# Binding eight partition-sum products into one row, and moving the keys' transposes, in a two-layer hybrid inference step

## The chip, the cores and the metric

The kernel runs on one core of one Trainium2 chip. The metric is the device time of one launch in microseconds (us). The program's matrix engine is called PE or TensorE here, its vector engine DVE or VectorE, its activation engine ACT, its fourth compute engine POOL; SP issues most transfers from the chip's memory.

## What is computed

Two layers are applied to 128 context tokens (g = 0) and 128 latent tokens (g = 1) of width 2048. Cut to what matters:

```python
# mod = silu(c) @ w_mod[l] + b_mod[l]: six segments of 2048 columns,
# for each of two conditioning vectors (context, latent)
shift1, scale1, gate1, shift2, scale2, gate2 = split(mod, 6)
h = rmsnorm(x, norm1) * (1 + scale1) + shift1
proj = h @ w_in            # attention q, k, v; linear attention q, k, v, gates
# attention: per-head RMS norm of q and k, rotary positions, softmax
# gated linear attention (GLA), forward and backward, in chunks
x = x + gate1 * (concat(att, gla) @ w_out)
h = rmsnorm(x, norm2) * (1 + scale2) + shift2
x = x + gate2 * (square(relu(h @ w_up)) @ w_down)
```

## The kernel before

**Main work.** Everything is float32. A weight matrix is worked on in blocks of 512 columns (`block`, lines 398 to 453); a block takes 256 rows of the weights at a time (a chunk). SP loads a chunk, ACT casts it to a rounded high part `wh` (line 131), DVE subtracts to get the low part `wl` (line 132; both are called `wx` where they live in a borrowed buffer), and PE adds three products per 128 rows and token group: lines 443, 444 and 445, the third being the only one that reads the low part. A chunk has twelve such main matmuls of 128x512. The results are finished by `done`, and other work is put between the chunks as `side` steps.

**Modulation.** The twelve segments of `mod` come from 12 matrices of 2048x2048, one column of which meets two conditioning vectors only. Most segments go through PE (`mod_pe`, line 293). Five are accumulated on DVE by `mod_dve` (lines 339 to 367): (0,5), (1,1), (1,0) and (1,2) during layer 0 and (1,5) during layer 1, written (layer, segment). For each half of the columns and each group of 128 rows, DVE multiplies the loaded block `rawm` by that row's conditioning value and adds it to two sums `ga` of 128x1024, one per token group (lines 355 and 357): 32 blocks, 64 such instructions a segment. The four sums lie in borrowed buffers QT, KT, BF, BB, which the next segment uses again. What is left is the sum over the partitions:

```python
for g in range(2):
    for q in range(4):
        nc.tensor.matmul(ps[32 * q:32 * q + 32, :], unit[:, 1 - g:33 - g],
                         acc[q // 2][g][:, (q % 2) * 512:(q % 2) * 512 + 512], start=g == 0, stop=g == 1)
```

Eight products of PE (line 364), each taking two passes, so 16 matmuls in the trace, with a 128x32 weight tile `unit` that puts the sum of group g into row g of a quarter of the result. q = 0, 1 belong to the first half of the columns, whose sums are complete 16 blocks earlier than those of q = 2, 3.

**Keys.** `kv_a` is called when a block of keys and values is finished, once for each token group; it norms and (for the latent tokens) rotates the keys `y` (lines 744 to 756, DVE and POOL), transposes them on PE (line 769, tile `kaT`) and copies the result with ACT into `kTp` or `kTs`, which the attention reads later. The block after that is the queries' projection `Q_A`, whose side steps are two levels of the GLA (`level`, line 708's small matmuls `sc`).

**Order.** Each engine has its own queue. Where nothing else is said, a scheduler in the compiler decides the order in it from a simulated timeline, so that an edit in one place can move instructions elsewhere. `tc.high_priority()` puts an instruction ahead of others that are ready; `after(x, others)` adds an order without a semaphore.

**The boundary of the layers.** After layer 0's last block, `norm` (lines 460 to 476) forms the next layer's input: a chain of one-column operations (`v` line 138 on DVE, `y` twice on ACT lines 140 and 141, `t` twice on DVE lines 143 and 144, `r` line 146), a diagonal tile `dg` (line 469), 16 products with it on PE (line 473, `xnT`), and evictions by `modulate` (`xv` lines 482 and 484, then high part TH and low part TL, lines 131 and 132). Layer 1's first matmuls read TH and TL.

Of the kernel before, what the change touches and what calls it, by code (L numbers as in the profile page):

```python
# [20 lines left out]
P = 128  # L21
# [6 lines left out]
Q_A, K_A, Q_G, K_G, V_G, O_G, R_F = 0, 1024, 1536, 2048, 2560, 3584, 4608  # L28
# [23 lines left out]
def trunk(tc, nc, I, O):  # L52
    with ExitStack() as st:
# [41 lines left out]
        def mtile(shape=(P, 512), name="m"):  # L95
            return ps_m.tile(list(shape), F32, tag="m", name=name)
# [171 lines left out]
        shared = [lambda: rawp.tile([P, 1024], F32, tag="raw", name="rawm")]  # L268


        main = []

        def mod_group(ps, todo, size, behind={}):

# [68 lines left out]
        def mod_dve(l, seg):  # L343
            acc = []
# [14 lines left out]
                    if half < 1 or kc < KC - 1:  # L359
                        yield 1  # L360
            ps = mtile((P, 512), "mod")
            for g in range(2):
                for q in range(4):
                    nc.tensor.matmul(ps[32 * q:32 * q + 32, :], unit[:, 1 - g:33 - g],  # L364
                                     acc[q // 2][g][:, (q % 2) * 512:(q % 2) * 512 + 512], start=g == 0, stop=g == 1)
            mod_columns(l, seg, ps, 1)
            yield 1

# [31 lines left out]
        def block(TH, TL, src, at=None, done=None, mods_per=0.0, chs=None, side=(), dve=None, early={}):  # L400
# [14 lines left out]
            for g, ch in order:  # L415
# [23 lines left out]
                for k in range(2):  # L439
                    kc = ch * 2 + k  # L440
                    first, final = ch == chs[0] and k == 0, ch == chs[-1] and k == 1
                    xh, xl = TH[:, kc, g * P:(g + 1) * P], TL[:, kc, g * P:(g + 1) * P]
                    nc.tensor.matmul(acc[g], xh, wh[:, k, :], start=first, stop=False)  # L443
                    nc.tensor.matmul(acc[g], xl, wh[:, k, :], start=False, stop=False)  # L444
                    m = nc.tensor.matmul(acc[g], xh, wl[:, k, :], start=False, stop=final)  # L445
                    if len(main) < 16:
                        main.append(m)
                if ch == chs[-1] and done is not None:
# [110 lines left out]
        for l in range(L):  # L559
# [203 lines left out]
                nc.scalar.copy(x, pt)  # L763

            def kv_a(g, y):
                x = qk_finish(y[:, 0:256], 2, 1, g)
                pt = mtile((P, 2, P), "kaT")
                for j in range(2):
                    nc.tensor.transpose(pt[:, j], x[:, j], ident)
                if g == 0:  # L770
                    store(O["new_cache_k"][0, l], x)
                    store(O["new_cache_v"][0, l], heads(y[:, 256:512]))
                    nc.scalar.copy(kTp, pt)
                else:
                    nc.scalar.copy(kTs[:, :, P:2 * P], pt)

            MH, ML = new_t()

# [32 lines left out]
            att = lambda g, kv: lambda: attend(g, kv, heads(QA[kv][:, g]), heads(KA[:, g, 256:512]))  # L811
            QA = [None, None]
            KA = proj(K_A, kv_a, side=lv[0:2])
            QA[0] = proj(Q_A, q_a, side=lv[2:4])
            in_turn(shared)
            mod_rate[0] = N_MOD["bc"[l]][1]
            QA[1] = proj(Q_A + 512, q_a, side=[att(0, 0), lv[4], att(1, 0), lv[5]])
# [215 lines left out]
```

## Time and profile before

| | |
|---|---|
| Time, median of 3 runs (lowest to highest) | 2346.33 us (2345.97 to 2348.18) |
| Profiled execution: its time, and the span of its records | 2340.4 us, 2338.6 us |
| Mean granted clock of TensorE | 0.993 |
| Busy: PE, DVE, ACT, POOL | 2294.8, 1629.2, 1091.2, 187.5 us |
| Read from memory, written | 601.01 MB, 10.03 MB |

Busy times count an engine's own instructions. A row of a timeline gives start, duration, engine, line, operation, out<-in, and behind it in brackets the idle time of that engine just before it and what ended that; matmuls follow each other in a pipeline, so their durations overlap, and the step from start to start is what one costs. "PEld" is PE's weight load.

### The profile page before, as it was taken

What the parts mean: (1) busy time and instruction counts of PE and PEld (TensorE: products, weight loads), DVE (VectorE), ACT (ScalarE), POOL (GpSimd) and SP (SyncE); (2) the same over time, 40 slices, a digit from 0 to 9 for tenths busy, and PEclk for the clock granted to TensorE, in tenths of its full rate; (3) what the DMA queues carried; (4) which work ended last, traced back from release to release, by engine and by line L of the source; (5) the groups of instructions that cost most, each with busy time, mean ns of one, the idle gap of its engine ahead of it and who ended that gap; (6) DMA issues with size and microseconds to landing.
All of it is one profiled execution on the core that took longest, in us unless ns stands there. A gap on an engine that the chain in (4) does not pass through costs nothing.

```text
span 2338.6 us, 34912 instructions
## 1 busy us (share of the span) xinstructions
PE 2294.8 (98%) x13603; PEld 1830.4 (78%) x13603; DVE 1629.2 (70%) x1935; ACT 1091.2 (47%) x1476; POOL 187.5 (8%) x260
## 2 busy tenths in 40 slices
PE   8999899999999999999999999999999999999998
PEld 5677577788788788788777677788888888888887
DVE  4656767589999999589874865567996454445455
ACT  4334446455445344435454554546544543543542
POOL 1001521000000000000010522010000000000010
PEclk8999999999999999999999999999999999999999
DMA  9999889869989898588887667776887656656673
GB/s 351 376 344 351 292 280 357 299 215 308 312 289 320 283 318 287 203 272 298 277 292 263 203 231 229 255 256 225 296 292 236 182 190 196 180 193 193 181 232 134
DMA packets 278374, 613.35 MB, mean 262 GB/s; under 512 B 24368, under 2 KB 32880, under 8 KB 278208
## 3 DMA queue, kind: packets, MB, share of 16 engines
q1 hardware_dynamic: 268128, 581.51, 73.6%
q0 software_dynamic: 9872, 29.53, 4.3%
q8 instruction: 107, 1.75, 0.3%
q14 instruction: 59, 0.48, 0.1%
q10 hardware_dynamic: 208, 0.08, 0.0%
HBM read 601.01 MB, written 10.03 MB: 261 GB/s over the span
## 4 chain that ended last, share of the span: by engine, by line
PE 90%; DMA 3%; issue 2%; DVE 2%; ACT 1%; POOL 0%; SPq 0%; POOLq 0%; DVEq 0%; ACTq 0%
PE acc L443 27%; PE acc L445 26%; PE acc L444 26%; PE mod L293 4%; DMA rawm<-in_w_mod_dram 2%; DMA bank<-in_w_mod_dram 1%; PE aT L125 1%; PE xnT L473 1%; PE sc L708 1%; PE mod L364 1%; DVE wl L132 1%; PE po L806 0%; PE op L869 0%; PE mod L239 0%; PE op L866 0%
## 5 line engine op out<-in xcount | busy, mean ns | idle before, releaser
L132 DVE TENSOR_TENSOR wl<-raw,wh 128x1024 fp32r<-128x1024 f32 (+1 forms) x586 | 692.1, 1189 | 429.3 <-ACT wh L131 421.4
L131 ACT CAST wh<-raw 128x1024 fp32r<-128x1024 f32 (+1 forms) x586 | 593.4, 1017 | 780.4 <-PE acc L444 673.1
L443 PE MATMUL acc<-wh,TH 128*128 128x512 f32 x2248 | 887.5, 395 | 5.5 <-ACT TH L131 3.1
L444 PE MATMUL acc<-wh,TL 128*128 128x512 f32 x2248 | 881.2, 392 | 0.1
L445 PE MATMUL acc<-wl,TH 128*128 128x512 f32 x2248 | 862.8, 394 | 0.3 <-DVE wl L132 0.3
L443 PEld LDWEIGHTS acc<-wh,TH 128*128 128x128 f32 x2248 | 423.6, 188 | 105.0 <-issue 10.3
L445 PEld LDWEIGHTS acc<-wl,TH 128*128 128x128 f32 x2248 | 422.5, 188 | 95.7 <-issue 6.2
L444 PEld LDWEIGHTS acc<-wh,TL 128*128 128x128 f32 x2248 | 423.7, 188 | 87.5 <-issue 1.1
L357 DVE SCALAR_TENSOR_TENSOR ga<-rawm,CT,ga 128x1024 f32<-128x1024 f32 x300 | 377.1, 1277 | 25.1 <-DMA rawm<-in_w_mod_dram 24.7
L132 DVE TENSOR_TENSOR wx<-raw,wx 128x1024 fp32r<-128x1024 f32 (+1 forms) x182 | 194.6, 1079 | 88.9 <-ACT wx L131 86.7
L131 ACT CAST wx<-raw 128x1024 fp32r<-128x1024 f32 (+1 forms) x182 | 168.3, 938 | 177.6 <-PE acc L444 144.7
L444 PE MATMUL acc<-wx,TL 128*128 128x512 f32 x632 | 246.1, 390 | 0.0
L443 PE MATMUL acc<-wx,TH 128*128 128x512 f32 x632 | 246.0, 389 | 0.0
L445 PE MATMUL acc<-wx,TH 128*128 128x512 f32 x632 | 239.5, 390 | 0.0
L445 PEld LDWEIGHTS acc<-wx,TH 128*128 128x128 f32 x632 | 118.7, 188 | 25.4 <-DVE wl L132 0.8
L443 PEld LDWEIGHTS acc<-wx,TH 128*128 128x128 f32 x632 | 118.6, 188 | 24.9
L444 PEld LDWEIGHTS acc<-wx,TL 128*128 128x128 f32 x632 | 118.7, 188 | 24.7
L227 POOL DMA_DIRECT2D gd<-gs x4 | 2.1, 522 | 844.4 <-DVE gs L226 844.4
L293 PE MATMUL mod<-bank,CT 128*32 128x256 f32 x992 | 65.9, 389 | 0.5 <-DMA bank<-in_w_mod_dram 0.5
L293 PE MATMUL mod<-rawm,CT 128*32 128x256 f32 x800 | 53.8, 388 | 6.1 <-DMA rawm<-in_w_mod_dram 6.1
L948 ACT ACTIVATE relu<-acc 128x512 f32<-128x512 f32 x64 | 37.9, 593 | 34.8 <-PE acc L445 34.8
L293 PEld LDWEIGHTS mod<-bank,CT 128*32 128x32 f32 x992 | 30.1, 111 | 27.0 <-issue 7.2
(256 smaller groups left out, 1389.9 us busy)
## 6 DMA issues: line engine op xcount, KB each, us to landing
rawm<-in_w_mod_dram SPq DMA_DIRECT2D x260, 512.0 KB, 5.3
raw<-in_w_up_dram SPq DMA_DIRECT2D x256, 512.0 KB, 4.5
raw<-in_w_down_dram SPq DMA_DIRECT2D x256, 512.0 KB, 5.3
raw<-in_w_in_dram SPq DMA_DIRECT2D x144, 512.0 KB, 6.5
bank<-in_w_mod_dram SPq DMA_DIRECT2D x124, 512.0 KB, 8.3
raw<-in_w_out_dram SPq DMA_DIRECT2D x64, 512.0 KB, 7.4
gx<-gd POOLq DMA_DIRECT2D x32, 256.0 KB, 6.7
x1d<-x POOLq DMA_DIRECT2D x16, 256.0 KB, 5.1
```

The lines of the kernel that those rows point to most:

```text
L125: turned.append(nc.tensor.transpose(dst[:, j], s, ident))
L131: a = nc.scalar.copy(hi, v)
L132: d = nc.vector.tensor_tensor(out=lo, in0=v, in1=hi.bitcast(F32), op=ALU.subtract)
L293: m = nc.tensor.matmul(ps[r:r + 32, c:c + 256], CT[:, 2 * kc:2 * kc + 32], part(raw), start=at not in seen, stop=left[at] == 0)
L357: nc.vector.scalar_tensor_tensor(out=ga[g], in0=raw, scalar=c, in1=ga[g], op0=ALU.mult, op1=ALU.add)
L364: nc.tensor.matmul(ps[32 * q:32 * q + 32, :], unit[:, 1 - g:33 - g], acc[q // 2][g][:, (q % 2) * 512:(q % 2) * 512 + 512], start=g == 0, s ...
L443: nc.tensor.matmul(acc[g], xh, wh[:, k, :], start=first, stop=False)
L444: nc.tensor.matmul(acc[g], xl, wh[:, k, :], start=False, stop=False)
L445: m = nc.tensor.matmul(acc[g], xh, wl[:, k, :], start=False, stop=final)
L473: nc.tensor.matmul(pts[j // 2][:, j % 2], xt[q][:, j * P:(j + 1) * P], dg, start=True, stop=True)
L708: nc.tensor.matmul(sps[hh][w_ * c:w_ * c + w_, n], EB[r, n % 4, j0:j0 + w_], EA[r, n % 4, i0:i0 + w_], start=True, stop=True, tile_positio ...
L948: nc.scalar.activation(r, acc, AF.Relu)
```

## The change

It does two things. In `mod_dve` the order of the eight products is turned round: group 1 comes first, with q from 3 down to 0, then group 0. The first of them, the head, reads the sum that is complete last; the other seven get a high priority and are ordered behind it. In `kv_a` the transposes and copies are taken out and put into a function `turn_keys`, which is the first side step of the `Q_A` block; its transposes are ordered behind the main matmul that was issued last when it is called.

```diff
-            for g in range(2):
-                for q in range(4):
-                    nc.tensor.matmul(ps[32 * q:32 * q + 32, :], unit[:, 1 - g:33 - g],
-                                     acc[q // 2][g][:, (q % 2) * 512:(q % 2) * 512 + 512], start=g == 0, stop=g == 1)
+            head = None
+            for g in (1, 0):
+                for q in (3, 2, 1, 0):
+                    with tc.high_priority() if head else nullcontext():
+                        m = nc.tensor.matmul(ps[32 * q:32 * q + 32, :], unit[:, 1 - g:33 - g],
+                                             acc[q // 2][g][:, (q % 2) * 512:(q % 2) * 512 + 512], start=g == 1, stop=g == 0)
+                    after(m, [head] if head else [])
+                    head = head or m
...
                     m = nc.tensor.matmul(acc[g], xh, wl[:, k, :], start=False, stop=final)
+                    last_main[:] = [m]
...
             def kv_a(g, y):
-                x = qk_finish(y[:, 0:256], 2, 1, g)
-                pt = mtile((P, 2, P), "kaT")
-                for j in range(2):
-                    nc.tensor.transpose(pt[:, j], x[:, j], ident)
+                keys.append(qk_finish(y[:, 0:256], 2, 1, g))
                 if g == 0:
-                    store(O["new_cache_k"][0, l], x)
+                    store(O["new_cache_k"][0, l], keys[0])
                     store(O["new_cache_v"][0, l], heads(y[:, 256:512]))
-                    nc.scalar.copy(kTp, pt)
-                else:
-                    nc.scalar.copy(kTs[:, :, P:2 * P], pt)
+            keys = []
+            def turn_keys():
+                for g, x in enumerate(keys):
+                    pt = mtile((P, 2, P), "kaT")
+                    for j in range(2):
+                        after(nc.tensor.transpose(pt[:, j], x[:, j], ident), last_main)
+                    nc.scalar.copy(kTs[:, :, P:2 * P] if g else kTp, pt)
...
-            QA[0] = proj(Q_A, q_a, side=lv[2:4])
+            QA[0] = proj(Q_A, q_a, side=[turn_keys] + lv[2:4])
```

The counts of instructions on every engine stay as they are. What moves is shown at three places; lines of the changed kernel are numbered a little higher (364 is 367 there, 443 to 445 are 448 to 450, 469 is 475, 708 is 714, 769 is 783, 974 is 984).

PE's order at the end of segment (0,5), before (`ga_5017`, `ga_5018` are the first half's sums, `ga_5693`, `ga_5694` the second's; the products with `ga_5017` stand some 210 rows further up):

```order
L444 MATMUL acc0_6041<-wh_6045,TL_4808 128x512
L364 MATMUL mod_6281<-ga_5693,unit_100 32x512 x2
L445 MATMUL acc0_6041<-wl_6046,TH_4807 128x512
L443 MATMUL acc0_6041<-wh_6045,TH_4807 128x512
L444 MATMUL acc0_6041<-wh_6045,TL_4808 128x512
L445 MATMUL acc0_6041<-wl_6046,TH_4807 128x512
L443 MATMUL acc0_6041<-wh_6067,TH_4807 128x512
L444 MATMUL acc0_6041<-wh_6067,TL_4808 128x512
L364 MATMUL mod_6281<-ga_5018,unit_100 32x512 x2
L364 MATMUL mod_6281<-ga_5694,unit_100 32x512 x2
L445 MATMUL acc0_6041<-wl_6068,TH_4807 128x512
```

and in the changed kernel:

```order
L448 MATMUL acc0_6041<-wh_6067,TH_4807 128x512
L449 MATMUL acc0_6041<-wh_6067,TL_4808 128x512
L367 MATMUL mod_6281<-ga_5694,unit_100 32x512 x2
L367 MATMUL mod_6281<-ga_5018,unit_100 32x512 x2
L367 MATMUL mod_6281<-ga_5693,unit_100 32x512 x2
L367 MATMUL mod_6281<-ga_5017,unit_100 32x512 x2
L448 MATMUL acc1_6042<-wh_6045,TH_4807 128x512
```

The eight products stand in one row, near the place where the last four stood. (1,1), (1,0) and (1,2) have their products in one row too; those of (1,5) stood in one row before as well. For (1,0) the row takes the place of the first two products, two blocks earlier than the last.

DVE's order at the layer boundary, before (`s1`, `v`, `t`, `r`, `dg` are the norm's chain for the context tokens; `wl_10788` and `wx_10862` are splits of later chunks, `acc2_5542` the latent tokens' residual):

```order
L132 TENSOR_TENSOR wl_10760<-raw_10757,wh_10759 128x512 x2
L138 TENSOR_SCALAR v_10514<-s1_10512 128x1
L132 TENSOR_TENSOR wl_10788<-raw_10785,wh_10787 128x512 x2
L974 TENSOR_TENSOR acc2_5542<-acc1_10381,acc2_5542 128x512
L132 TENSOR_TENSOR wx_10862<-raw_10859,wx_10861 128x512
L143 TENSOR_TENSOR t_10519<-y_10516 128x1
L132 TENSOR_TENSOR wx_10862<-raw_10859,wx_10861 128x512
L977 TENSOR_TENSOR acc2_5542<-acc2_5542,gx_10377 128x512
L144 SCALAR_TENSOR_TENSOR t_10519<-t_10519,v_10514 128x1
L978 TENSOR_TENSOR acc2_5542<-acc2_5542,gx_10377 128x512
L146 SCALAR_TENSOR_TENSOR r_10522<-t_10519,y_10516 128x1
L469 TENSOR_SCALAR dg_10524<-ident_94,r_10522 128x128
```

and in the changed kernel:

```order
L132 TENSOR_TENSOR wl_10760<-raw_10757,wh_10759 128x512
L138 TENSOR_SCALAR v_10514<-s1_10512 128x1
L132 TENSOR_TENSOR wl_10760<-raw_10757,wh_10759 128x512
L143 TENSOR_TENSOR t_10519<-y_10516 128x1
L144 SCALAR_TENSOR_TENSOR t_10519<-t_10519,v_10514 128x1
L146 SCALAR_TENSOR_TENSOR r_10522<-t_10519,y_10516 128x1
L475 TENSOR_SCALAR dg_10524<-ident_94,r_10522 128x128
L132 TENSOR_TENSOR wl_10788<-raw_10785,wh_10787 128x512 x2
L984 TENSOR_TENSOR acc2_5542<-acc1_10381,acc2_5542 128x512
L490 TENSOR_SCALAR xv_10532<-xnT_10526,modc1_163 128x128 x2
```

Four half splits and the three steps of the latent tokens' residual (lines 974, 977, 978), which stood inside the chain, now stand behind `dg` and between the evictions `xv`. On ACT the two `y` stand ahead of the cast of `wh_10787` instead of behind it.

PE's order at layer 1's keys, before (`kaT` for the context tokens, then for the latent tokens; `sc` are a level's small products):

```order
L444 MATMUL acc_11602<-wh,TL 128x512
L769 MATMUL kaT<-ident,y 128x128 x2
L445 MATMUL acc_11602<-wl,TH 128x512
L708 MATMUL sc<-EA,EB 32x32 x25
L769 MATMUL kaT<-ident,y 128x128 x2
L708 MATMUL sc<-EA,EB 32x32 x39
L443 MATMUL acc_11601<-wh,TH 128x512
L444 MATMUL acc_11601<-wh,TL 128x512
```

and in the changed kernel, where the first `kaT` stands six rows above the first row shown (between them one main matmul of the chunk before and the first four of a new one):

```order
L450 MATMUL acc_11593<-wl,TH 128x512
L448 MATMUL acc_11593<-wh,TH 128x512
L449 MATMUL acc_11593<-wh,TL 128x512
L450 MATMUL acc_11593<-wl,TH 128x512
L450 MATMUL acc_11594<-wl,TH 128x512
L448 MATMUL acc_11594<-wh,TH 128x512
L449 MATMUL acc_11594<-wh,TL 128x512
L450 MATMUL acc_11594<-wl,TH 128x512
L714 MATMUL sc<-EA,EB 32x32 x6
L783 MATMUL kaT<-ident,y 128x128 x2
L714 MATMUL sc<-EA,EB 32x32 x58
L448 MATMUL acc_11593<-wh,TH 128x512
```

A chunk of twelve main matmuls stands between the two `kaT`, and 6 instead of 25 of the `sc` instructions. Layer 0's keys keep their place in PE's order. Behind layer 1's keys the order is the same on every engine.

One more move has no rows here: on DVE, 22 accumulations of segment (1,2), which stood behind 1010 us of the trace of before, stand in the changed kernel among the splits of the stretch from 965 us on, behind the row of (1,0).

## Rows read from the trace of the kernel before

**Rows 1.** The page of the profile: busy time of each engine with its share of the span.

```profile
PE 2294.8 (98%) x13603; PEld 1830.4 (78%) x13603; DVE 1629.2 (70%) x1935; ACT 1091.2 (47%) x1476; POOL 187.5 (8%) x260
```

**Rows 2.** What TensorE (PE) waited for in the whole span: engine, line, releaser: us in total, times, longest.

```profile
PE xnT L473 <- DVE dg L469: 6.8, 3, 4.2
...
PE kaT L769 <- DVE y L756: 3.1, 1, 3.1
```

**Rows 3.** PE's timeline around four of the fourteen groups of line 364's matmuls (start, us, engine, line, op, out<-in, tile, shape, xcount; one record is one pass): the first group, with main matmuls ahead of it and behind it, one of eight, the second of segment (1,2) and the one of layer 1's segment (1,5).

```profile
590.32 0.39 PE L443 MATMUL acc<-wh,TH 128*128 128x512 f32 x1
590.55 0.39 PE L444 MATMUL acc<-wh,TL 128*128 128x512 f32 x1
590.86 1.05 PE L364 MATMUL mod<-ga,unit 128*32 128x512 f32 x4
592.18 0.40 PE L444 MATMUL acc<-wh,TL 128*128 128x512 f32 x1
...
643.14 1.07 PE L364 MATMUL mod<-ga,unit 128*32 128x512 f32 x8
...
1155.77 1.91 PE L364 MATMUL mod<-ga,unit 128*32 128x512 f32 x12
...
2205.64 1.93 PE L364 MATMUL mod<-ga,unit 128*32 128x512 f32 x16
```

**Rows 4.** Line 364 by itself: the weight loads of its products (x80), durations in ns, minimum/median/maximum.

```profile
L364 PEld LDWEIGHTS mod<-ga,unit x80: 106/109/111, 590.9 to 2206.5; 128*32 128x32 f32 x80
```

**Rows 5.** VectorE's (DVE's) timeline: the last accumulation (line 357) of segment (0,5) and the split behind it.

```profile
634.50 1.28 DVE L357 SCALAR_TENSOR_TENSOR ga<-rawm,CT,ga 128x1024 f32<-128x1024 f32 x1
635.69 1.22 DVE L132 TENSOR_TENSOR wl<-raw,wh 128x1024 fp32r<-128x1024 f32 x1
```

**Rows 6.** Timeline of all engines: three splits of a weight chunk on DVE (line 132), each with the first matmul on PE that reads it.

```profile
780.67 1.22 DVE L132 TENSOR_TENSOR wl<-raw,wh 128x1024 fp32r<-128x1024 f32 x1
...
782.23 0.39 PE L445 MATMUL acc<-wl,TH 128*128 128x512 f32 x1
...
804.49 1.21 DVE L132 TENSOR_TENSOR wl<-raw,wh 128x1024 fp32r<-128x1024 f32 x1
...
806.91 0.40 PE L445 MATMUL acc<-wl,TH 128*128 128x512 f32 x1
...
999.11 1.22 DVE L132 TENSOR_TENSOR wl<-raw,wh 128x1024 fp32r<-128x1024 f32 x1 [1.50 <-ACT wh L131]
...
1006.66 0.39 PE L445 MATMUL acc<-wl,TH 128*128 128x512 f32 x1
```

**Rows 7.** Windows: busy us of PE, PEld, DVE, ACT and POOL in a stretch (instructions), then PE's granted clock, DMA share, GB/s.

```profile
700.00:840.00 140.00, 140.00 (x634) 113.31 (x634) 133.23 (x126) 61.13 (x67) 0.00 (x0) 1.00 0.89 306
965.00:1010.00 45.00, 45.00 (x204) 35.74 (x202) 23.84 (x22) 16.88 (x16) 0.00 (x0) 1.00 0.57 181
1345.00:2336.00 991.00, 984.95 (x5301) 803.47 (x5299) 595.75 (x674) 465.73 (x607) 52.52 (x84) 1.00 0.68 218
```

**Rows 8.** What DVE waited for between 600 and 800 us (us in total, times, longest).

```profile
DVE ga L357 <- DMA rawm<-in_w_mod_dram: 10.2, 12, 1.9
```

**Rows 9.** Timeline of all engines at the layer boundary: the norm's chain for the context tokens (v, y, y, t, t, r, dg), what stands in it, and the first matmuls behind.

```profile
1210.72 0.15 DVE L138 TENSOR_SCALAR v<-s 128x1 f32<-128x1 f32 x1
...
1211.05 1.14 ACT L131 CAST wh<-raw 128x512 fp32r<-128x512 f32 x2 [1.28 <-issue]
...
1211.70 1.29 DVE L132 TENSOR_TENSOR wl<-raw,wh 128x512 fp32r<-128x512 f32 x2 [0.83 <-ACT wh L131]
...
1212.10 0.20 ACT L140 ACTIVATE y<-v 128x1 f32<-128x1 f32 x1
...
1216.30 0.29 DVE L469 TENSOR_SCALAR dg<-ident,r 128x128 f32<-128x128 f32 x1
...
1216.73 4.54 PE L473 MATMUL xnT<-dg,acc 128*128 128x128 f32 x24 [4.18 <-DVE dg L469]
...
1217.46 0.73 DVE L484 TENSOR_SCALAR xv<-xnT,modc 128x128 f32<-128x128 f32 x2 [0.87 <-PE xnT L473]
...
1219.55 0.68 DVE L132 TENSOR_TENSOR TL<-xv,TH 128x512 fp32r<-128x512 f32 x1
...
1221.71 0.47 PE L444 MATMUL acc<-wh,TL 128*128 128x512 f32 x1
```

**Rows 10.** Timeline of all engines at layer 1's keys: a split on DVE, and PE.

```profile
1328.43 1.22 DVE L132 TENSOR_TENSOR wl<-raw,wh 128x1024 fp32r<-128x1024 f32 x1
...
1330.02 0.64 PE L708 MATMUL sc<-EA,EB 64*32 64x32 f32 x50
...
1333.78 0.66 PE L769 MATMUL kaT<-ident,y 128*128 128x128 f32 x2 [3.12 <-DVE y L756]
...
1335.37 0.79 PE L443 MATMUL acc<-wh,TH 128*128 128x512 f32 x1
...
1337.16 0.40 PE L444 MATMUL acc<-wh,TL 128*128 128x512 f32 x1
```

**Rows 11.** PE's timeline some 20 us earlier, where a short wait ends.

```profile
1311.92 1.22 PE L708 MATMUL sc<-EA,EB 64*32 64x32 f32 x120 [0.95 <-DVE ST L715]
```

**Rows 12.** Windows (columns as in rows 7): the stretch behind that wait, and the one at the keys.

```profile
1313.00:1316.60 3.60, 3.60 (x25) 2.79 (x12) 3.60 (x3) 3.12 (x7) 3.34 (x2) 0.53 1.04 419
1334.00:1336.00 2.00, 2.00 (x82) 1.51 (x82) 0.76 (x1) 0.96 (x3) 0.39 (x1) 0.50 0.58 184
```

More of the change, by code (lines that the diff above doesn't have):

```diff
@@ L268, in trunk @@
         shared = [lambda: rawp.tile([P, 1024], F32, tag="raw", name="rawm")]
-        main = []
+        main, last_main = [], []
         def mod_group(ps, todo, size, behind={}):
```

## The prediction

> **What bounds the kernel.** I read the page first: PE is busy for 98% of the span [rows 1]. So a change pays if it shortens PE's queue or one of PE's waits, and only where nothing else takes the time back. Then I asked what PE waits for. Two waits concern this change: `dg` at a layer boundary, 4.2 us at its longest, and the latent keys `y`, 3.1 us in one piece [rows 2]. Then I looked at line 364's own matmuls, which are PE work of a peculiar price, and last at the stretches around them, to see whether PE alone sets the pace there.
>
> **The price of a group.** From the main matmul at 590.55 to the one at 592.18 there are 1.63 us with a group of four between them; main matmuls follow each other in 0.23 us (590.32 to 590.55), so two of these steps make 0.46 and the group costs 1.17 [rows 3]. A group of eight takes as long as one of four (1.07 against 1.05 us); groups of twelve and sixteen take 1.91 and 1.93 [rows 3], 0.87 more, so 2.05. PE thus pays by groups rather than by matmuls. In order of time the fourteen groups are 4, 4, 8 for segment (0,5); 4, 8, 4 for (1,1); 4, 6, 6 for (1,0); 4, 12 for (1,2); 16 for (1,5).
>
> **Part 1, the row of eight.** Three groups cost 3.51, one row 2.05: 1.46 saved at each of the first three segments. At (1,2) 1.17 + 2.03 becomes 2.05: 1.15. At (1,5) nothing changes. Together 5.5 us of PE work, if every row finds its sums ready. The head waits for the last sum: at (0,5) that ends at 635.78 [rows 5], and the row stands near 643.14, so there are over 7 us to spare; at the others the row stands behind the last sum as well by the order of DVE's rows. What is queued behind a waiting head would be all of PE's main work, so this would hurt if it happened; I put it at nothing.
>
> What takes some of it back is DVE. Between 700 and 840 us it is busy for 133.2 of 140 us beside a PE that is busy throughout [rows 7]: both are nearly bounds there. Its split of 780.67 ends at 781.89 and is read at 782.23, 0.34 us later; that of 804.49 ends at 805.70 and is read at 806.91, 1.21 later [rows 6]. The change takes one accumulation (1.28 long [rows 5]) from ahead of the first split, but PE would arrive there some 2.6 us early (three groups and the first of the next three gone, one row added) and wait about 1 us. At the second split, PE can be early by 1.21 at most, unless DVE gets early itself. So of the 2.9 us of the first two segments I keep **1.2**. Upper bound 2.9 (DVE's 10.2 us of waits for `rawm` loads [rows 8] shrink and DVE moves along); lower bound 0. The other two segments keep 1.46 + 1.15 = **2.6**.
>
> The stretch from 965 to 1010 needs a word. DVE is busy for only 23.8 of 45 us [rows 7], and 22 accumulations of segment (1,2) move into it: at 1.2 us from start to start ([rows 5]: 634.50 to 635.69) 26.4, against 21.2 idle, so DVE falls behind by 5.2. The splits have a lead of 6.3 us (999.11 + 1.22 = 1000.33 against 1006.66 [rows 6]), which covers this with about 1 us left. Cost: nothing, but the cover is thin; it is rival C. Behind 1010 DVE has that much less to do.
>
> **Part 2, the layer boundary (nobody asked for it, the scheduler moved it).** Before, `v` ends at 1210.87, but ACT first casts two halves (1211.05, 1.14 long) and `y` begins at 1212.10; DVE then has splits and residuals between the steps, and `dg` comes at 1216.30, so PE stands still for 4.18 us [rows 9]. In the new order one half split (0.65) remains in the chain: `v` 1210.87, two `y` of 0.2, two `t`, `r` and `dg`, each some 0.2 behind the other: `dg` is there at about 1212.4, when PE ends its last main matmul. That is an upper bound of 4.2. But the work that left the chain now stands before the evictions on DVE: from 1212.4 two half splits 1.29, a residual 0.65, `xv` 0.7, two half splits 1.3, a residual 0.65, two more `xv` pairs 1.4, then TL 0.68 (sizes from [rows 9], about 0.65 for those of 128x512): TL is there at 1219.1, where the matmul that reads it began at 1221.71 [rows 9]. Net **2.6**; lower bound 0.9, if two of the displaced splits wait for their casts as the one at 1211.70 did (0.83 [rows 9]).
>
> **Part 3, the keys.** In layer 0 PE's order is unchanged: nothing. In layer 1 PE waits 3.12 us for the latent keys, behind 50 passes of `sc` (0.64 us) [rows 10]. Now twelve main matmuls stand ahead of the wait (12 x 0.227 = 2.7 us) and 19 of the 25 `sc` instructions behind it (0.5 us): the wait shrinks to 3.12 - 2.7 + 0.5 = 0.9, and 2.2 is saved. The split of that chunk ended at 1329.65 [rows 10]; it would now be read from about 1331 on. Beyond that there is the clock. The five main matmuls from 1335.37 to 1337.16 take 1.79 us in place of 1.13 [rows 10]; they and the `sc` ahead of them ran at a granted clock of 0.50 [rows 12], the lower of the two levels (1.2 GHz). If a wait of 0.9 leaves the clock at 2.4 GHz, up to 0.9 more is saved. The nearest row speaks against it: behind a wait of 0.95 among `sc` matmuls [rows 11] it was 0.53 [rows 12]. So I take **2.2**, bounds 1.5 (the 0.7 that the lower clock cost on five main matmuls falls on as many more) and 3.1. Nothing is queued behind the moved ACT copies that anyone waits for at once: the attention reads `kTp` and `kTs` a block later.
>
> **Sum.** 1.2 + 2.6 + 2.6 + 2.2 = 8.6 us. Behind 1345 PE is busy for 985 of 991 us at full clock [rows 7] and the order there is the same, so what is gained goes to the end. The profiled execution took 2340.4 us and would take 2331.8; the median of the runs lies 5.9 above it (2346.3), so I forecast **2337.7**. A measurement of this kernel tells a difference from none at about 0.2%, 4.7 us: faster means under 2341.6.
>
> **A rule that speaks against the row.** The sixteen passes of [rows 3] took 1.93 us, while their sixteen weight loads take 0.109 each [rows 4], 1.74 together: they lie beside the matmuls. The Trainium skill, "TensorE: Matmul & The Clock Gate", section "Part 3: Packing small matmuls — row/col tiling", says that a weight load overlaps running matmuls only when its row group differs; here all eight products use all rows. By it, as an estimate, the loads would add 1.74 to a row, and the rows would cost 1.4 us more in all, not 5.5 less. The trace disagrees with it for this very row, so as a rival (2342.9: parts 2 and 3 less 1.4) it gets 0.01.
>
> **Rivals.**
> A, the forecast: 0.62.
> B, VectorE becomes the bound wherever a row is saved: PE's gains at the first three segments are all waited away at splits. For it: the leads of 0.34 and 1.21. Against it: a DVE that is half idle from 965 to 1010. Left are 1.2 of (1,2), 2.6 and 2.2: 6.0, so 2340.3. Chance 0.16.
> D, the change does not do what it is there for, or its accident: the scheduler's order at the boundary gains nothing, because loads or casts hold the chain (6.0 left, 2340.3), or the keys give nothing as well (3.8 left, 2342.5). For it: ACT idled 1.28 us before the cast at 1211.05 for no reason that the trace names [rows 9]. Chance 0.15.
> C, slower: from 965 to 1010 DVE takes eleven `rawm` loads that were spread out before, and each split behind a late load is late for PE. Between 600 and 800 DVE waited 12 times for such loads, 0.85 us on average and 1.9 at most [rows 8]. With 1.9 each, 20.9 less 1 of lead: 2337.7 + 19.9 = 2357.6. At 0.85 each it costs 8.3 and the kernel is as fast as before; it is slower by over 0.2% from 1.3 a load. Against it: the DMA engines are busy for 0.57 there, 0.89 between 700 and 840 [rows 7]. Chance 0.06.
>
> **The numbers.** Faster: nearly all of A (0.60), most of B at 2340.3 (0.10), a third of D (0.05): 0.75. Slower: the far part of C, 0.05. Same: 0.20. For the range, all best bounds give 2.9 + 2.6 + 4.2 + 3.1 = 12.8 less, 2333.5; the worst cases of B and D give 2342.5. I take 2333 to 2343; C and a little on either side lie outside.
>
> **What would show it.** PE's timeline must have five groups of 16 of about 1.93 us and no others; a wait for a sum ahead of one of them would prove me wrong on the head. PE's waits for `wl` on DVE should come to 1 or 2 us between 700 and 840 and to none from 965 to 1015; many there is B or C. The wait for `dg` of 4.2 should be gone, part of it coming back as waits for TL or a free tile; the wait for `y` at the keys should be under 1 us. If PE shows no new wait and the time is still above 2341, the mistake is in the price of the groups.

## The result, and the profile after

The changed kernel takes 2334.15 us (median of 7 runs, 2328.08 to 2342.45), the kernel before 2346.33 (7 runs, 2341.81 to 2350.13). The ratio is 0.995, 95% interval 0.9938 to 0.9962: by it 11.7 us less, between 8.9 and 14.5 (the medians differ by 12.2). The forecast was 8.6 us less, 2337.7, in a range of 2333 to 2343: the right direction, the time inside the range but only 1.2 us above its lower end, the gain 3 us short.

The two profiled executions differ by 2.2 us only (spans 2336.4 and 2338.6). Why that is so little is the first thing to settle. The page of the changed kernel, beside [rows 1]:

```profile
span 2336.4 us, 34921 instructions
...
PE 2293.1 (98%) x13603; PEld 1832.8 (78%) x13603; DVE 1629.0 (70%) x1935; ACT 1090.6 (47%) x1476; POOL 188.7 (8%) x260
```

What PE waits for in the changed kernel, beside [rows 2]; of the 2.7 us that are left for `dg`, 2.4 belong to a norm of layer 0, at some 480 us, and are there before the change too:

```profile
...
PE acc L450 <- DVE wl L132: 3.8, 4, 1.7
...
PE xnT L479 <- DVE dg L475: 2.7, 2, 2.4
...
PE kaT L783 <- DVE y L762: 0.7, 1, 0.7
...
PE acc L449 <- DVE TL L132: 0.5, 1, 0.5
...
```

Since PE runs 8640 main matmuls in each kernel, the n-th one that starts is a landmark, and the time between two landmarks can be compared stretch by stretch. This is the main reading of what follows. The table gives microseconds longer (+) or shorter (-) than the first execution of the kernel before, by stretches of that execution; every row is one profiled execution, and the kernels named in it are explained under the experiments:

```
              30-584  584-699  699-837  960-1030  1135-1202  1202-1249  1309-1328  1328-1352  1352-end
before again   +8.21     0.00    +3.59      0.00       0.00      +0.57       0.00      +1.53     +0.23
changed        +6.69    -1.49    +3.51     -1.53      -1.14      -4.22      +0.02      -3.64     +0.25
  again        +5.20    -1.49    +1.02     -1.53      +0.23      -4.14      -0.01      -3.67     +0.02
  third        +4.88    -1.49    +2.29     -1.53      +0.40      -4.22      +0.01      -3.67     -0.12
rows only      +5.67    -1.49    -1.28     -1.53      -1.15      -3.28      +0.03      +0.35     -0.36
keys only      +3.12     0.00    +1.11      0.00       0.00       0.00      -0.01      -3.67     -0.11
boundary only  +8.60     0.00     0.00      0.00       0.00      -3.35      +0.03      +0.36     +0.25
row order      +7.07    -1.47    +0.60     -1.51      -0.79      -4.16      +0.03      -3.67     -0.05
rows late      +4.61     0.00    +0.67     -1.53      -0.79      -3.77      -0.45      -4.05     +0.01
keys later     +6.33    -1.48    -0.09     -1.53      -0.55      -4.05      +1.48      -4.42     +0.27
O x3, raw x7  +18.63    -1.51    -1.53     -1.54      -1.15      -3.66      +0.03      -3.64     +9.32
E buffers      +5.12    -1.53    -1.59     -1.53      -1.15      -4.03      -0.01      -3.63     -0.03
  again        +6.15    -1.53    -1.59     -1.53      -0.69      -3.77      +0.03      -3.68      0.00
```

The stretches left out (837 to 960, 1030 to 1135, 1249 to 1309) differ by 0.13 at most, the first 30 us by 1.1. Three things are to be seen. First, the stretches at 584, 960 and 1309 us repeat to a few hundredths in most executions, and so does the one at 1328 where the keys are moved as in the change (all but rows late); those at 1135 and 1202 scatter by some 1.5 and 1 us. Second, the first 584 us do not repeat: the first execution of the kernel before was 3 to 9 us faster there than every other one with eight weight buffers, its own repetition among them (+8.21). That hides the gain between the two profiles, and it is the likely source of the 5.9 us between that execution and the median; only one other execution of the kernel before was profiled. Third, 699 to 837 scatters, from 0 to +3.6 in the old order and from -1.3 to +3.5 in the new one, unless `rawm` has more buffers (-1.5 to -1.6).

The rows. PE's timeline at the rows of (0,5), (1,1) and (1,0), with the main matmuls around the first, beside [rows 3]:

```profile
646.38 0.39 PE L449 MATMUL acc<-wh,TL 128*128 128x512 f32 x1
646.70 1.92 PE L367 MATMUL mod<-ga,unit 128*32 128x512 f32 x16
648.55 0.50 PE L448 MATMUL acc<-wh,TH 128*128 128x512 f32 x1
648.90 0.40 PE L449 MATMUL acc<-wh,TL 128*128 128x512 f32 x1
...
797.77 1.92 PE L367 MATMUL mod<-ga,unit 128*32 128x512 f32 x16
...
971.53 1.92 PE L367 MATMUL mod<-ga,unit 128*32 128x512 f32 x16
```

There are five such rows and no other group of line 367. From 646.38 to 648.90 there are 2.52 us; less two steps of 0.23 between main matmuls this leaves 2.06, where the forecast had 2.05.

Where a row's gain was lost again, between 699 and 837, DVE's timeline in the changed kernel:

```profile
704.62 1.22 DVE L132 TENSOR_TENSOR wl<-raw,wh 128x1024 fp32r<-128x1024 f32 x1
708.39 2.48 DVE L357 SCALAR_TENSOR_TENSOR ga<-rawm,CT,ga 128x1024 f32<-128x1024 f32 x2 [2.55 <-DMA rawm<-in_w_mod_dram]
710.78 1.22 DVE L132 TENSOR_TENSOR wx<-raw,wx 128x1024 fp32r<-128x1024 f32 x1
711.92 1.22 DVE L132 TENSOR_TENSOR wl<-raw,wh 128x1024 fp32r<-128x1024 f32 x1
714.24 2.48 DVE L357 SCALAR_TENSOR_TENSOR ga<-rawm,CT,ga 128x1024 f32<-128x1024 f32 x2 [1.10 <-DMA rawm<-in_w_mod_dram]
716.64 2.35 DVE L132 TENSOR_TENSOR wl<-raw,wh 128x1024 fp32r<-128x1024 f32 x2
```

and what PE does meanwhile:

```profile
717.91 0.50 PE L450 MATMUL acc<-wl,TH 128*128 128x512 f32 x1 [1.67 <-DVE wl L132]
```

The accumulation at the head of DVE's queue waits 2.55 and then 1.10 us for its load. The splits stand behind it in the queue and run one after another without a gap once it is done, so they wait too; PE stands still until the first of the two at 716.64 is done.

The layer boundary, beside [rows 9] (timeline of DVE, ACT and PE):

```profile
1215.26 0.15 DVE L138 TENSOR_SCALAR v<-s 128x1 f32<-128x1 f32 x1
...
1215.44 0.20 ACT L140 ACTIVATE y<-v 128x1 f32<-128x1 f32 x1 [0.30 <-DVE v L138]
...
1216.50 0.29 DVE L475 TENSOR_SCALAR dg<-ident,r 128x128 f32<-128x128 f32 x1
...
1217.03 1.29 DVE L132 TENSOR_TENSOR wl<-raw,wh 128x512 fp32r<-128x512 f32 x2 [0.24 <-ACT wh L131]
...
1217.54 0.39 PE L450 MATMUL acc<-wx,TH 128*128 128x512 f32 x1
...
1217.76 3.55 PE L479 MATMUL xnT<-dg,acc 128*128 128x128 f32 x28
...
1222.06 0.71 PE L479 MATMUL xnT<-dg,acc 128*128 128x128 f32 x4 [0.45 <-DVE xv L490]
...
1222.56 0.68 DVE L132 TENSOR_TENSOR TL<-xv,TH 128x512 fp32r<-128x512 f32 x1
...
1223.30 0.50 PE L449 MATMUL acc<-wh,TL 128*128 128x512 f32 x1 [0.52 <-DVE TL L132]
```

`dg` is ready at 1216.79, before PE has begun its last main matmul (1217.54). PE goes on without a wait, 28 of the 32 passes of the products in 3.55 us where 24 took 4.54, and pays 0.45 and 0.52 for the evictions later.

That 28 take less time than 24 is the clock, which the forecast did not count at this place. Windows (columns as in rows 7) of the kernel before, behind its wait of 4.18 us, and of the changed kernel:

```profile
1218.00:1220.00 2.00, 2.00 (x12) 2.00 (x11) 1.29 (x4) 1.68 (x4) 0.00 (x0) 0.50 1.05 315
1220.00:1222.00 2.00, 2.00 (x13) 1.94 (x13) 1.56 (x5) 1.86 (x5) 0.00 (x0) 0.75 0.93 283
```

```profile
1219.00:1221.00 2.00, 2.00 (x18) 1.81 (x17) 2.00 (x5) 1.91 (x6) 0.00 (x0) 1.00 0.96 298
```

From 1218 to 1220, behind the wait, the granted clock is at the lower of its two levels (1.2 GHz), and it rises again before 1222; in the changed kernel, without the wait, it stays at the upper one (2.4 GHz). From the first of these passes to the next main matmul there are 0.18 us a pass before (24 from 1216.73 to 1221.03) and 0.12 after (28 in 3.35). As an estimate, some 1.4 us of the old kernel's time here (24 x 0.06) were the low clock.

The keys of layer 1, beside [rows 10] (PE's timeline) and [rows 12] (windows):

```profile
1330.62 0.38 PE L783 MATMUL kaT<-ident,y 128*128 128x128 f32 x2
...
1333.91 0.28 PE L714 MATMUL sc<-EA,EB 64*32 64x32 f32 x12
1334.84 0.44 PE L783 MATMUL kaT<-ident,y 128*128 128x128 f32 x2 [0.66 <-DVE y L762]
1335.21 0.99 PE L714 MATMUL sc<-EA,EB 64*32 64x32 f32 x93
```

```profile
1334.00:1336.00 2.00, 1.34 (x107) 1.06 (x109) 1.97 (x4) 1.20 (x2) 0.00 (x0) 1.00 0.73 250
```

The wait is 0.66 in place of 3.12, which is 2.46 us, and the granted clock in that stretch is 1.00 in place of 0.50. The stretch 1328 to 1352 gains 3.63 to 3.68 us in every execution with the keys placed as in the change but one (rows late, 4.05), so the other 1.2 of it are put down to the clock.

### The profile page after: what moved, and what is told of

The parts are those of the page before. It is cut to its first block, busy times and chain, and to the rows that moved or that the text cites. A ratio compares the mean times of both kernels' runs of the same rounds, so it can differ in the third digit from the quotient of the medians.

```text
span 2336.4 us, 34921 instructions
## 1 busy us (share of the span) xinstructions
PE 2293.1 (98%) x13603; PEld 1832.8 (78%) x13603; DVE 1629.0 (70%) x1935; ACT 1090.6 (47%) x1476; POOL 188.7 (8%) x260
## 4 chain that ended last, share of the span: by engine, by line
PE 88%; DMA 4%; DVE 3%; issue 3%; ACT 0%; SPq 0%; POOL 0%; POOLq 0%; DVEq 0%
PE acc L448 26%; PE acc L449 26%; PE acc L450 26%; PE mod L293 4%; DMA rawm<-in_w_mod_dram 2%; DMA bank<-in_w_mod_dram 1%; PE aT L125 1%; DVE wl L132 1%; PE xnT L479 1%; PE sc L714 1%; DVE ga L357 1%; PE po L815 0%; PE op L876 0%; SPq L284 0%; PE mod L367 0%
```

## Experiments

**The two halves apart.** The kernel before with the new order of the eight products alone ("rows only"), and with `turn_keys` alone ("keys only"); the edits are the two halves of the diff above.

> Only the row of eight, keys as before. Measured by stages on PE's timeline (main matmul by main matmul against the kernel before). Theory: 1.5 us gained at segment (0,5), nothing kept between 700 and 840 us because DVE and its loads of rawm set the pace there (PE waits for wl of 2 to 4 us appear), 1.5 at (1,0) and 1.2 at (1,2), 4.2 at the layer boundary, whose order this part alone moves; keys +-0.3. Total 5 to 7 us under the kernel before. Rival (the waits for wl in the changed kernel's profile were late loads of that one execution): no waits for wl, 5.5 us gained between 590 and 1200, total 9.7. Rival (boundary belongs to the keys' part): boundary unchanged, total 1 to 3.

> Only the keys' transposes moved, the partition sums as before. Theory: nothing moves before the keys of layer 1, the boundary keeps its wait of 4.2, the wait for y falls from 3.1 to 0.7 and the clock stays up: 3.6 us gained there (2.4 of wait, 1.2 of clock), total 3 to 4 us under the kernel before. Rival (the forecast: the clock falls all the same): 2.2.

Measured: rows only 2337.06 us, ratio 0.9957 (0.9945 to 0.997); keys only 2342.44, ratio 0.9979 (0.9971 to 0.9988). So both halves gain, about 10 and 5 us; together that is 15, more than the whole (11 on this chip, below), but the intervals are 4 to 6 us wide, and the stretches tell more. The boundary belongs to the rows' half alone (-3.28 against 0.00). It gains there what the changed kernel gains, some 4.2; two waits of PE for `bank` loads behind it (0.8 us, at 1225 to 1240) take the rest back. The keys' half gains 3.67 at 1328 to 1352 and nothing elsewhere. Its wait there, on PE:

```profile
1337.88 0.44 PE L778 MATMUL kaT<-ident,y 128*128 128x128 f32 x2 [0.66 <-DVE y L757]
```

For rows only, the expectation for 699 to 837 failed in this execution: no wait for `wl`, and 1.28 of the 1.5 were kept. Its total of 5 to 7 us failed with it; the rival's 9.7 is near. Rows only also shows something else. PE's timeline from 1306 on:

```profile
1306.67 0.27 PE L713 MATMUL sc<-EA,EB 64*32 64x32 f32 x8 [0.77 <-ACT EA L689]
1307.89 1.22 PE L713 MATMUL sc<-EA,EB 64*32 64x32 f32 x120 [0.95 <-DVE ST L720]
...
1315.76 0.50 PE L450 MATMUL acc<-wl,TH 128*128 128x512 f32 x1 [1.44 <-DVE wl L132]
```

and the windows behind these waits, in rows only, then in the first and in the third execution of the changed kernel, where the waits end at 1313.05 and 1312.12:

```profile
1309.00:1313.00 4.00, 4.00 (x29) 3.30 (x18) 4.00 (x3) 3.92 (x8) 3.78 (x3) 1.00 1.02 413
```

```profile
1313.00:1316.60 3.60, 3.55 (x125) 3.04 (x126) 3.57 (x2) 2.93 (x5) 2.70 (x3) 0.60 1.03 422
```

```profile
1313.00:1316.00 3.00, 3.00 (x52) 2.50 (x39) 3.00 (x3) 2.94 (x6) 2.54 (x2) 1.00 1.02 412
```

The two short waits are those of [rows 11], but in rows only the clock stays at 1.00, where it was 0.53 before [rows 12]. That gains 1.6 us, and a wait of 1.44 for a split takes it back: the stretch 1309 to 1328 comes out even. Half clock there had cost nothing, because DVE was next in line. The changed kernel does the same thing both ways: its first execution falls to 0.60 behind these waits, its third stays at 1.00 and waits 1.43 for the split, and the stretch is even in both.

**The changed kernel again.**

> The changed kernel once more. Theory (DVE and its loads bound 700 to 840): PE waits for wl there again, 2 to 4 us in all, and from 590 us to the end 8 us are gained against the kernel before. Rival (late loads of one execution): the waits for wl fall under 1 us and 10 to 11 us are gained from 590 to the end. The first 590 us, where PE's order is the same, may differ by several us either way. The ratio of times should come out near 0.995 again.

Measured: 2336.39 us, ratio 0.9952 (0.9939 to 0.9966). 9.55 us are gained from 584 on, 8.21 in the first execution; between 590 and 1030 PE waited for `wl` once (1.5 us). This lies between theory and rival: late loads are part of it, but the stretch 699 to 837 loses something in most executions.

**The boundary alone.** The kernel before, with the order at the boundary forced:

```diff
+                            after(a, chain["act"] if ch in (4,) else [])
+                            after(d, chain["dve"] if ch in (4,) else [])
...
+            i = nc.vector.tensor_scalar_mul(dg, ident, r)
+            if l == 1 and which == 0 and g == 0:
+                chain["dve"], chain["act"] = [i], ys[-1:]
...
+                        i = nc.vector.tensor_tensor(out=y, in0=acc, in1=y, op=ALU.add)
+                        after(i, chain["dve"])
```

> The kernel before, with nothing but the order at the layer boundary forced: the splits and casts of one later chunk and the latent tokens' residual behind dg. Theory: the wait of 4.2 us for dg goes, 3.5 to 4.3 us are gained there, the rest as before, total 4 us less. Rival (the displaced work comes back as waits for TL, as the forecast counted): 2 to 2.8 gained. Rival (PE has mains enough to fill the wait whatever DVE does, the gain belongs to PE's order): under 1.

Measured: 2343.73 us, ratio 0.9987 (0.9977 to 0.9996), about 3 us. The stretch gains 3.35, a little under the 3.5 to 4.3 of the theory, and the wait for `dg` is gone; what PE waits for between 1200 and 1360:

```profile
PE kaT L774 <- DVE y L761: 3.1, 1, 3.1
PE acc L448 <- DVE wl L133: 1.4, 1, 1.4
...
PE acc L447 <- DVE TL L133: 0.5, 1, 0.5
```

So the order of some ten rows on DVE and ACT is worth 3.4 us, with no row of eight and no moved key in the kernel. Of the 4.2 us at the boundary 3.4 are shown to be that order, and a side effect of the change; the forced order is not the changed kernel's in every row (20 passes follow each other here, 28 there), and what brings the other 0.9 was not tested.

**What a row costs.** The changed kernel with the two loops swapped:

```diff
-            for g in (1, 0):
-                for q in (3, 2, 1, 0):
+            for q in (3, 2, 1, 0):
+                for g in (1, 0):
```

> The changed kernel with the eight products of a row in another order: for each quarter q first group 1, then group 0, so that the products of one column tile stand next to each other. In the traces so far the passes of a row start in sets of four, 7 ns apart, one on each column tile, and the sets 0.43 to 0.46 us apart. Theory (a row costs the passes on one column tile one behind the other, and the tiles run beside each other only if neighbours in the queue lie on different tiles): a row of 16 takes 5 to 6 us in place of 1.93, about 3.7 us more at each of five rows, 12 to 19 us more in all (part of it hidden where PE waits for DVE). Rival (a row has a fixed price, or PE takes the passes out of order): 1.9 to 2.1 a row and the time of the changed kernel.

Measured: 2337.23 us, ratio 0.9954 (0.9941 to 0.9968). The row at (0,5), PE's timeline:

```profile
646.99 0.39 PE L449 MATMUL acc<-wh,TL 128*128 128x512 f32 x1
647.31 1.95 PE L367 MATMUL mod<-ga,unit 128*32 128x512 f32 x16
649.19 0.50 PE L448 MATMUL acc<-wh,TH 128*128 128x512 f32 x1
```

1.95 us: my theory fell, the order inside a row makes a difference of 0.03. The single records show how the price comes about: in the changed kernel passes start at 646.701, .708, .715, .721, then from 647.154, 647.583 and 648.012 on in fours; here at 647.312, .326, .339, .352, 13 ns apart and not 7, then again in fours 0.43 to 0.45 us later. So passes start four at a time in either order, and a row of sixteen is four such steps. In the kernel before, a group of four started its passes in twos (590.864, .871, then 591.319, .325), a group of six in threes, a group of eight in fours: two steps each, and that is why they cost the same. The group of twelve started 4, 4, 2 and 2: four steps, as many as sixteen. That group has the quarters q = 2 and 3 twice and 0 and 1 once, the groups of four, six and eight have none twice, and a full row has all four twice; so the steps are two for each product on the quarter that has the most of them. The prices 1.17 and 2.05 then split into 0.44 a step and 0.29 a group, and the 1.46 of a bound row into two steps (six become four) and two groups less.

**Undoing the first two rows.** (0,5) and (1,1) in the old order, unbound:

```diff
+            bound = (l, seg) not in ((0, 5), (1, 1))
-            for g in (1, 0):
-                for q in (3, 2, 1, 0):
+            for g in ((1, 0) if bound else (0, 1)):
+                for q in ((3, 2, 1, 0) if bound else (0, 1, 2, 3)):
...
-                    head = head or m
+                    if bound:
+                        head = head or m
```

> The changed kernel with the rows at (0,5) and (1,1) unbound again (their products in the old order, free to be placed); (1,0), (1,2) and the keys as changed. Theory (what PE saves before 840 us is mostly lost again while DVE waits for rawm loads between 700 and 840): 0 at 584 to 699 us in place of -1.5, between 0 and +1 at 699 to 837, from 840 on as in the changed kernel, boundary included; the total within 1.5 us of the changed kernel. Rival (the rows keep their 3 us): 3 us slower than the changed kernel, ratio to the kernel before 0.9965 or more.

Measured: 2336.77 us, ratio 0.9951 (0.9939 to 0.9964), the same as the changed kernel. The 1.5 us of the row at (0,5) are missing at 584 to 699, as the theory had it; the total, within a few us, cannot show them. The boundary's order is there without these two rows, so a later one is enough for it.

**The kernel before again.**

> The kernel before, profiled once more. Theory (the profiled execution that stood for it in the forecast was an early one: its loads in the first 590 us came well): 30 to 584 us takes 3 to 9 us longer than in that execution, as in every other kernel here with the same order there; from 584 on nothing differs but 699 to 837 (0 to +1.2). Rival (the order of these kernels does something to the first 590 us): 30 to 584 within 1 us of the first execution.

Measured: one run, 2353.77 us. 30 to 584 took 8.21 us longer, so the first execution was an early one, as the theory had it. 699 to 837 took 3.59 longer, with PE waiting for splits in the old order too, more than I had expected of it:

```profile
PE acc L445 <- DVE wl L132: 2.2, 2, 1.9
```

The expectation that nothing else differs failed at two places, 0.57 longer at the boundary and 1.53 at the keys. The waits there are the same 4.2 and 3.1 us; what is longer is the low clock behind them: main matmuls behind the keys start every 0.43 us over seven more steps than in the first execution, where they are back at 0.23 from 1337.16 on (granted clock 0.50 from 1347 to 1351 here). Against this execution the change gains that much more at both places.

**More buffers for `rawm`.** First three buffers O, with one fewer for weights; then, with all eight left, every second block of three segments in a buffer E:

```diff
-RAW_BUFS = 8
+RAW_BUFS = 7
-        BIG = {..., "O": 2, ...}
+        BIG = {..., "O": 3, ...}
```

```diff
-                    raw = big("O", name="rawm")
+                    raw = big("E" if kc % 2 and (l, seg) in ((0, 5), (1, 1), (1, 0)) else "O", name="rawm")
```

> The changed kernel with three buffers for rawm instead of two, and seven for the weight chunks instead of eight (there is no room for both). Theory (DVE's queue is held up at its head by rawm loads that can be issued only when one of two buffers is free): DVE's waits for rawm between 590 and 1030 fall from 17 us to under 8, no waits of PE for wl, and 699 to 837 keeps its 1.3 to 1.5 us: 2 to 4 us faster than the changed kernel. Rival (the DMA engines are the bound in that stretch, or weight chunks come late with seven buffers): waits as before or new ones for raw, same time or slower by several us.

> The changed kernel with every second rawm block of (0,5), (1,1) and (1,0) in a buffer of the four named E, which no one uses at that time, and all else, the eight weight buffers too, as changed. Theory (two buffers for rawm hold up DVE's queue): DVE's waits for rawm from 590 to 1030 fall from 13 to 18 us to under 6, no wait of PE for wl there, 699 to 837 keeps 1.5 us, the first 590 us and the stretch from 1352 on as in the changed kernel: 0 to 4 us faster than it, ratio to the kernel before 0.994 to 0.995. Rival (the third buffer of the other experiment helped only because fewer weight loads ran ahead and left the DMA engines to rawm): waits of 8 us and more, 699 to 837 as in the changed kernel.

Measured: with seven weight buffers 2353.0 us, ratio 1.002 (1.001 to 1.0029), slower by 0.2%, where the theory had a gain. But 699 to 837 comes out at -1.53, and DVE's wait for `rawm` from 590 to 1030, 18.2 us in the changed kernel, is

```profile
DVE ga L357 <- DMA rawm<-in_w_mod_dram: 3.5, 3, 1.5
```

The loss is elsewhere: +18.6 us in the first 584, where the other executions stand at +3 to +9, and 9.3 behind 1352. Behind 1352 PE waits 2.2 and 2.5 us for `dg` and `xv`, in the changed kernel 0.2 for `dg` and nothing for `xv`, so the scheduler's order moved as well; how much of the loss is the missing weight buffer's was not tested. With E buffers 2331.04 us, ratio 0.9943 (0.9929 to 0.9956), and 699 to 837 at -1.59. The gain of a row is kept when two buffers no longer hold up DVE's queue. This is shown by the E buffers, since the edit changes nothing else; the scheduler only places a few small products of other work a little earlier or later there.

**The two side by side.**

> The changed kernel, for the comparison with the one with E buffers on the same chip. Theory: as before, ratio near 0.995; from 584 on the deterministic stretches as in its other executions (-1.5 at 584 to 699, -1.5 at 960 to 1030, -4.1 at the boundary, -3.65 at the keys), 699 to 837 anywhere from -1.3 to +3.6. Rival: a row's gain or the keys' differ by over 0.3 us from the earlier executions.

> The changed kernel with E buffers for every second rawm block, once more, on the same chip as the changed kernel. Theory: 699 to 837 at -1.5 again with waits for rawm under 3 us; 1.5 to 4 us faster than the changed kernel beside it. Rival (its five runs were early ones by chance): same time as the changed kernel within 1 us.

Measured on one chip: changed kernel 2336.17 us, ratio 0.9946 (0.9934 to 0.9959); E buffers 2333.0, ratio 0.9936 (0.9922 to 0.9949). DVE's wait for `rawm` from 590 to 1030, in the changed kernel and with E buffers:

```profile
DVE ga L357 <- DMA rawm<-in_w_mod_dram: 17.4, 19, 2.9
```

```profile
DVE ga L357 <- DMA rawm<-in_w_mod_dram: 1.1, 1, 1.1
```

The version with E buffers beats the kernel before clearly. Against the changed kernel it is 3 us ahead in the medians, and the intervals overlap, so by the times alone the gain is not shown; the stretch 699 to 837 (-1.59 twice, against +2.29, +1.02 and +3.51) is what separates them.

**The keys one step later.**

```diff
-            QA[0] = proj(Q_A, q_a, side=[turn_keys] + lv[2:4])
+            QA[0] = proj(Q_A, q_a, side=[lv[2], turn_keys, lv[3]])
```

> The changed kernel with the keys' transposes as the second side step of the queries' projection instead of the first. Theory (the wait for y of 0.7 us is what is left there, and y has been ready for long one side step later): no wait for y, 0.7 to 1 us less at the keys, the rest as in the changed kernel: about 1 us faster than it, not to be told from it by the clock. Rival (the step makes something else late, a buffer of the transposes or the first attention step behind it): a wait of another name of 1 to 3 us at 1330 to 1400.

Measured: 2338.15 us, ratio 0.9964 (0.9952 to 0.9976): nothing gained. PE's timeline:

```profile
1318.66 0.50 PE L450 MATMUL acc<-wl,TH 128*128 128x512 f32 x1 [1.42 <-DVE wl L132]
1334.61 0.44 PE L783 MATMUL kaT<-ident,y 128*128 128x128 f32 x2 [1.45 <-DVE y L762]
```

The wait for `y` did not go, it grew to 1.45; a wait for a split precedes it, which the third execution of the changed kernel has too. Why `y` came later, in the timeline of POOL and DVE:

```profile
1331.58 1.28 POOL L687 TENSOR_TENSOR EA<-BB 128x512 f32<-128x512 f32 x1
1331.66 1.48 DVE L761 TENSOR_TENSOR y<-y,rt 128x256 f32<-128x256 f32 x1 [1.06 <-POOL rot L759]
1333.17 1.38 DVE L762 TENSOR_TENSOR y<-y,rot 128x256 f32<-128x256 f32 x1
```

The last two steps of `y` took 1.48 and 1.38 us, where each took 0.42 or 0.43 in the changed kernel. Beside them POOL worked on `EA`, which it reached only behind them (1335.65 in the third execution) with the keys in the first side step. That POOL's work is the cause is likely from this, but was not tested by itself.

## Why the prediction was right, point by point

- **The price of a row: right.** 2.06 measured, 2.05 forecast; 1.49, 1.53 and 1.15 us gained at (0,5), (1,0) and (1,2), the last where no load came late, forecast 1.46, 1.46 and 1.15. No row waited for a sum. "By groups rather than by matmuls" was not the whole of it: PE pays by steps and by groups, as the records under "What a row costs" show, and the groups at hand gave the same prices either way. The rule of the Trainium skill, "TensorE: Matmul & The Clock Gate", section "Part 3: Packing small matmuls — row/col tiling", by which loads of the same row group would lie between the matmuls, does not hold for these column tiles: rows of 1.92 to 1.95 us with sixteen loads of 0.11. The rival built on it charged these loads to the new rows only; by its rule the old groups, with the same sixteen loads, would have paid them too.
- **VectorE takes part of it back: right in kind.** Of 2.9 us at the first two segments I kept 1.2. Kept were 1.49 at (0,5); at 699 to 837 the mean of six executions with the bound row and two buffers is +1.0, that of five with the old order +1.1 (before, before again, keys only, boundary only, rows late). So the row at (1,1) shows no gain within a scatter of some 1.5 us. The cause is one step further back than I put it: not the leads of 0.34 and 1.21 as such, but `rawm` loads that find no free buffer, at the head of DVE's queue.
- **Rival C did not come.** 960 to 1030 gives -1.51 to -1.54 in every execution with the row at (1,0) bound, and the executions of the changed kernel have no wait of PE for a split there.
- **The layer boundary: mechanism right, size off.** 2.6 forecast, 4.1 to 4.2 measured. The count from `dg` to the first use of TL held: 6.5 us (1216.79 to 1223.30) for 6.7. What I missed is that the chain also moved ahead of PE: `dg` was ready 0.75 us before PE's last main matmul began, where I had it 0.2 behind its begin (1 us), and that all 32 passes of the products stand ahead of the first use of TL, where four stood behind it before (0.4). I also took the old kernel's 1221.71 for that use as it stood and did not see that the low clock behind the wait was in it.
- **The keys: size off.** 2.2 forecast, 3.66 measured. The wait was 0.66 for a forecast of 0.9, and the clock did not fall. I took the nearest row ([rows 11, 12]) as evidence that it would; rows only shows the same two waits with the clock at 1.00, and the changed kernel shows them with 0.60 in one execution and 1.00 in another, so that row did not carry the conclusion. What lets it fall there in one execution and not in another of the same program stays open. I also priced the clock too low, 0.9 at most for 1.2 measured: from 1335.37 to 1337.16 there are four main matmuls and not five.
- **The sum.** By the stretches of the table, with the means where they scatter: 1.5 + 0 + 1.5 + 0.6 + 4.2 + 3.7 = 11.5 us; timed 11.7 (8.9 to 14.5). The forecast's 8.6 lacks 1.6 at the boundary and 1.5 at the keys; 0.6 for 1.15 at (1,2) and 1.5 for 1.2 at the first two segments nearly cancel. So close a sum is partly luck: it goes by one execution of the kernel before, the first 584 us are left out as scatter, and the other profiled execution would add 2.1 at the boundary and the keys.

## What to carry to other kernels

Compare two traces of a long kernel by landmarks of the bounding engine rather than by their spans: one execution's luck in its first quarter hid 6 of the 8.2 us that were gained behind it. When a scheduler decides the order, read what the edit moved far away: the largest single gain here lay some 60 us behind the last moved row, in rows nobody had edited. And where a queue is held up by a load at its head, look at that load's buffers before shortening its neighbours: the row at (1,1) kept its 1.5 us in each of three executions with more buffers, and on average nothing with two.

## What the runs showed that I had not expected

A group's price goes by steps 0.43 to 0.45 us apart, in each of which up to four passes start, and for a full row the order of the products does not matter. The clock of PE can be at half for 3 us and cost nothing, when another engine's wait would take its place (1309 to 1328); behind the 4.18 us at the boundary it did cost. And a version that gave `rawm` a third buffer and took one from the weights came out 16 us behind the changed kernel, though it removed most of the waits that it was made against.
